# Hybrid decoder step on one core: inverses of four systems joined by products over a block diagonal, and decoding-state updates as one split product per head pair

## The chip, the cores and the metric

One core of a Trainium2 chip runs the whole kernel as one launch. The metric is the device time in microseconds. The numbers of before are three runs of the kernel, and one execution taken by the hardware profiler.

## The reference

One inference step of a decoder layer for a prompt of 1024 tokens and for 8 decoding sequences of one token each (1032 columns, d_model 2048). One input projection feeds four groups of heads (A gated delta rule, B RWKV-7, C forgetting attention over a paged cache, D causal pooling); their gated outputs go through one output projection and a layer norm. All in fp32. Two parts matter here.

In the prompt, A and B are computed in 16 chunks of 64 tokens for 8 heads each, and each chunk and head needs the inverse of a unit lower triangular 64x64 matrix (in the reference a triangular solve):

```python
tri = lower + eye
u = lax.linalg.triangular_solve(tri, vb, left_side=True, lower=True)
```

For the decoding sequences each head has a 64x64 state, decayed and then changed by outer products: one term for A (key x new value), two for B (key x value, and a x the state's reading).

```python
S = (S * w_t[:, :, None, :] + s_kk[..., :, None] * (kk_t * a_t)[:, :, None, :]
     + v_t[..., :, None] * k_t[:, :, None, :])
```

## The kernel before

The projections are products in a split format: each fp32 operand is split into a part rounded to the F32R format and a remainder, and three products per tile are accumulated (`mm3`, L308 to L310; "split format" below). 57 column tiles are projected one after the other, 16 k-tiles deep, in three column groups of 344.

All other work is written as generators that are *fillers* (`add`, `fill`): after each quarter of a tile's k-tiles (36 matmuls of the projection) every filler is advanced by its rate, so a `yield` is where a filler hands back to the projection. What a step issues is then ordered by the framework, which simulates a timeline and places each instruction on its engine's in-order queue where its operands are ready by that simulation; so a filler's product can end up behind projection matmuls that were written after it. DMAs issued as `nc.sync` share the SP queue, in order.

`inverses` (L1192) handles a branch in two pairs of head pairs (four heads, 16 chunks each), through `invert` (L1134). The 64x64 matrix is cut into 32x32 blocks. The two diagonal blocks of 4 heads and 16 chunks are loaded with (block, chunk) on the 128 partitions, inverted by 31 elimination steps on VectorE (L1155 to L1162, seven yields), and written to the operand tensor in DRAM (AOP or BOP). Then for each head, 4 per pair, the off-diagonal block -D1 C D0 is made: Uc and Ct are loaded with rows on 32 partitions, Uc is transposed by VectorE (L1176), 16 fp32 products of 32x32 with 32 rows (L1179), a negated copy by ScalarE (L1180), 16 more products (L1183), a copy (L1185) and the stores, one of them zeros. A *block* in this text is such a run of 16 products. Branch B's inverses and then its decoding step (`start_b`) run beside the projection of the A tiles, branch A's inverses (`cached`) beside that of the first C tiles, where `chain_b` runs as well.

`state_step` (L1421) decays the states (128 partitions for two heads, 8 sequences x 64 columns, for each of 4 head pairs), and for each term transposes key and value to rows (L1435, 8 partitions), spreads the value rows to a block diagonal over the 8 sequences (L1446), and multiplies in fp32: per head pair two products of 8 rows, 64 columns of weights and 512 streamed columns (L1447). VectorE adds the result to the states (L1448). It runs for B beside the A projection (tag "k", one PSUM buffer), for A in the second pass of the output projection (`sample_a`, tag "b", two buffers).

Other lines that the prediction names: L997 is decode's product of cached keys (weights 128x32, four column groups of the array, 256 streamed columns); L1504 and L1505 are a head sum in the split format (128 rows, 128 columns of weights, 512 streamed); L463 and L479 are small products of A's preparation.

Of the kernel before, what the change touches and what calls it, by code (L numbers as in the profile page):

```python
# [179 lines left out]
class Kernel:  # L180
# [953 lines left out]
    def invert(self, pool, br, pair):  # L1134
# [4 lines left out]
        ld = self.ld[br]  # L1139

# [5 lines left out]
        for hp in (2 * pair, 2 * pair + 1):  # L1146
            for hb in range(4):
                r = slice(32 * hb, 32 * hb + 32)
                b = slice(32 * (hb % 2), 32 * (hb % 2) + 32)
                nc.sync.dma_start(L[16 * q:16 * q + 16], ld[hp, r, :, b].rearrange("j c i -> c j i"))  # L1150
                dst[q] = OP[:, r, hp, off + b.start:off + b.stop]
                q += 1
        nc.gpsimd.memset(U, 0.0)
# [11 lines left out]
        for hp in (2 * pair, 2 * pair + 1):  # L1165
            X = self.t(pool, [128, 16, 32], "ivX", bufs=1)
            T1 = self.t(pool, [128, 16, 32], "ivT", bufs=1)
            Uc = self.t(pool, [128, 16, 32], "ivC", bufs=1)
            Ct = self.t(pool, [128, 16, 32], "ivD", bufs=1)
            f2 = lambda a: a.rearrange("p a b -> p (a b)")  # L1170
            for hh in range(2):
                p0, p1 = slice(64 * hh, 64 * hh + 32), slice(64 * hh + 32, 64 * hh + 64)
                nc.sync.dma_start(Uc[p0], OP[:, p0, hp, off:off + 32].rearrange("c p i -> p c i"))
                nc.sync.dma_start(Uc[p1], OP[:, p1, hp, off + 32:off + 64].rearrange("c p i -> p c i"))
                nc.sync.dma_start(Ct[p0], ld[hp, p0, :, 32:64])
                nc.vector.transpose(f2(T1[p0]), f2(Uc[p0]))  # L1176
                ps = self.ps("k")
                for c in range(16):
                    nc.tensor.matmul(ps[p1, 32 * c:32 * c + 32], lhsT=Ct[p0, c], rhs=T1[p0, c], start=True, stop=True)  # L1179
                nc.scalar.activation(f2(X[p1]), ps[p1], AF.Copy, scale=-1.0)  # L1180
                ps = self.ps("k")
                for c in range(16):
                    nc.tensor.matmul(ps[p0, 32 * c:32 * c + 32], lhsT=X[p1, c], rhs=Uc[p1, c], start=True, stop=True)  # L1183

                nc.scalar.copy(f2(T1[p0]), ps[p0])  # L1185
                nc.sync.dma_start(OP[:, p0, hp, off + 32:off + 64].rearrange("c p i -> p c i"), T1[p0])
                nc.gpsimd.memset(T1[p1], 0.0)
                nc.sync.dma_start(OP[:, p1, hp, off:off + 32].rearrange("c p i -> p c i"), T1[p1])
                yield True


    def inverses(self, br, **side):  # L1192
        with self.tc.tile_pool(reuse_waits="tile", name="inv" + br, bufs=1, **side) as pool:
            for pair in range(2):
                yield from self.invert(pool, br, pair)
# [226 lines left out]
    def state_step(self, pool, St, dec, terms, out, tag):  # L1422

        nc = self.nc
        blk = self.ident[0:8, 0:8].unsqueeze(2).to_broadcast([8, 8, 64])
        f = lambda a: a.rearrange("p b d -> p (b d)")
        for hp in range(4):
            nc.vector.tensor_tensor(St[:, hp], St[:, hp], dec[:, hp].unsqueeze(2).to_broadcast([128, 8, 64]), op=ALU.mult)
        yield True
        for k, v in terms:  # L1430
            kv = []
            for i, x in enumerate((k, v)):
                ps = self.ps(self.stag)
                for hp in range(4):
                    nc.tensor.transpose(ps[0:8, 128 * hp:128 * hp + 128], x[:, hp], self.ident)  # L1435
                r = self.t(pool, [128, 512], f"srow{i}", bufs=1)[0:8]
                nc.scalar.copy(r, ps[0:8])
                kv.append(r)
            kr, vr = kv
            yield True  # L1440
            for hp in range(4):
                ps = self.ps(self.stag)
                for hh in range(2):
# [489 lines left out]
```

## Time and profile before

| | |
|---|---|
| median of 3 runs | 2431.46 us (2424.43 to 2431.7) |
| profiled execution | 2431.75 us, span 2430.0 us, mean granted TensorE clock 0.979 |
| TensorE (PE) busy | 2330.0 us, 96% of the span, 18324 matmul records |
| weight loads (PEld) | 2055.6 us, 85% |
| VectorE (DVE) | 1371.7 us, 56% |
| ScalarE (ACT) | 940.3 us, 39% |
| GpSimd (POOL) | 298.8 us, 12% |
| HBM read and written | 314.56 MB and 83.62 MB, 164 GB/s over the span |

PE is TensorE's matmuls; they are pipelined, so the recorded durations of neighbours overlap, and the busy time of a group is the time in which at least one of its records ran. L12 is line 12 of the kernel. An entry like `k<-ivT,ivD` is tile written <- tiles read; `32*32` is rows x columns of the weights, `32x32` the streamed operand. "Idle before" is the time in which the engine did nothing just before those instructions, with what it waited for.

### The profile page before, as it was taken

The page shows a single profiled execution, that of the slowest core. Times are in us where ns is not written, and L with a number is a line of the kernel's source. Part 1 is how long each engine was busy: PE and PEld are TensorE (multiplying, and loading weights), DVE is VectorE, ACT ScalarE, POOL GpSimd, SP SyncE. Part 2 cuts the span into 40 slices and gives each one's busy share as a digit, 9 for nine tenths or more (in the row PEclk, how much of TensorE's full clock was granted, in tenths as well). Part 3 has the DMA queues.
Part 4 walks back from the last instruction along what each step waited for, and adds up shares of the span by engine and source line. Part 5 has one row for each costly group of instructions (what it writes and reads, how often), then busy time and mean ns, then how long its engine had stood idle before and what let it go on. Part 6 is the DMA issues. An engine that isn't in the chain of part 4 may idle for free. (4 is left out here: it accounts for less than half of the span.)

```text
span 2430.0 us, 48607 instructions
## 1 busy us (share of the span) xinstructions
PE 2330.0 (96%) x18324; PEld 2055.6 (85%) x18324; DVE 1371.7 (56%) x2677; ACT 940.3 (39%) x1861; POOL 298.8 (12%) x416
## 2 busy tenths in 40 slices
PE   8999999999999999999999999999999989999984
PEld 8999999999988999897777777999855579878984
DVE  4665667777465567522222244554588654564598
ACT  5644445434443444221111122553466665201244
POOL 0000000000000000112112111100122110100175
PEclk9999999999999999999999999999999999999997
DMA  6233433545432345878888888553398785783312
GB/s 215 52 107 88 111 87 93 150 92 111 109 79 66 92 105 127 181 191 259 268 266 280 278 282 300 187 159 79 111 277 240 230 299 161 216 299 116 91 65 87
DMA packets 368388, 401.46 MB, mean 165 GB/s; under 512 B 203853, under 2 KB 227326, under 8 KB 367386
## 3 DMA queue, kind: packets, MB, share of 16 engines
q1 hardware_dynamic: 306418, 262.78, 36.8%
q10 hardware_dynamic: 50056, 101.60, 14.9%
q0 software_dynamic: 11680, 33.99, 4.1%
q8 instruction: 144, 2.36, 0.4%
q14 instruction: 90, 0.74, 0.1%
HBM read 314.56 MB, written 83.62 MB: 164 GB/s over the span
## 5 line engine op out<-in xcount | busy, mean ns | idle before, releaser
L308 PE MATMUL pj<-xh,wlo 128*128 128x344 f32 x2688 | 875.2, 327 | 9.6 <-DVE wlo L303 8.2
L309 PE MATMUL pj<-xl,whi 128*128 128x344 f32 x2688 | 871.6, 324 | 0.0
L310 PE MATMUL pj<-xh,whi 128*128 128x344 f32 x2688 | 867.1, 324 | 0.0
L308 PEld LDWEIGHTS pj<-xh,wlo 128*128 128x128 f32 x2688 | 508.9, 189 | 38.2 <-issue 18.6
L309 PEld LDWEIGHTS pj<-xl,whi 128*128 128x128 f32 x2688 | 509.5, 190 | 19.0 <-issue 13.6
L310 PEld LDWEIGHTS pj<-xh,whi 128*128 128x128 f32 x2688 | 508.6, 190 | 16.7 <-issue 13.4
L302 ACT CAST whi<-raw 128x256 fp32r<-128x256 f32 (+1 forms) x504 | 213.0, 424 | 751.8 <-PE pj L310 515.6
L303 DVE TENSOR_TENSOR wlo<-raw,whi 128x256 fp32r<-128x256 f32 (+1 forms) x504 | 224.6, 448 | 393.0 <-ACT whi L302 380.3
L308 PE MATMUL o<-gh,wlo 128*128 128x344 f32 x576 | 184.9, 325 | 3.2 <-ACT gh L1662 2.6
L309 PE MATMUL o<-gl,whi 128*128 128x344 f32 x576 | 187.0, 325 | 0.0
L310 PE MATMUL o<-gh,whi 128*128 128x344 f32 x576 | 186.5, 324 | 0.0
L308 PEld LDWEIGHTS o<-gh,wlo 128*128 128x128 f32 x576 | 108.2, 189 | 26.1 <-DVE y L1687 8.5
L309 PEld LDWEIGHTS o<-gl,whi 128*128 128x128 f32 x576 | 109.6, 190 | 3.9 <-issue 2.5
L310 PEld LDWEIGHTS o<-gh,whi 128*128 128x128 f32 x576 | 109.8, 191 | 3.3 <-issue 3.3
L365 ACT ACTIVATE stg<-pj 128x344 f32<-128x344 f32 x168 | 74.7, 457 | 90.2 <-PE pj L310 89.1
L997 PE MATMUL k<-dkv,dqb 128*32 128x256 f32 x1024 | 90.6, 394 | 13.4 <-DMA dkv<-in_ck 12.9
L1687 DVE TENSOR_TENSOR y<-y,o 128x344 f32<-128x344 f32 x96 | 48.3, 509 | 68.0 <-PE o L310 67.8
L861 DVE TENSOR_TENSOR cpl<-cpt,cph 128x512 fp32r<-128x512 f32 (+1 forms) x96 | 61.7, 660 | 16.2 <-ACT cph L860 15.4
L1105 PE MATMUL k<-dkv,dpT 128*8 128x512 f32 x512 | 69.8, 621 | 0.4 <-DMA dkv<-in_cv 0.4
L308 PE MATMUL o<-gh,wkl 128*128 128x392 f32 (+2 forms) x192 | 63.8, 332 | 0.3 <-DVE wkl L303 0.2
L310 PE MATMUL o<-gh,wkh 128*128 128x392 f32 (+2 forms) x192 | 63.6, 331 | 0.0
L309 PE MATMUL o<-gl,wkh 128*128 128x392 f32 (+2 forms) x192 | 63.3, 330 | 0.0
(594 smaller groups left out, 3405.9 us busy)
## 6 DMA issues: line engine op xcount, KB each, us to landing
dkv<-in_ck SPq DMA_DIRECT2D x256, 256.0 KB
dkv<-in_cv SPq DMA_DIRECT2D x256, 256.0 KB
raw<-in_w ACTq DMA_DIRECT2D x228, 256.0 KB
out_pj<-stg ACTq DMA_DIRECT2D x33, 516.0 KB
bop<-bop SPq DMA_DIRECT2D x16, 1024.0 KB
raw<-in_wo ACTq DMA_DIRECT2D x64, 256.0 KB
aop<-aop SPq DMA_DIRECT2D x16, 768.0 KB
aop<-aost SPq DMA_DIRECT2D x40, 256.0 KB
```

The costliest lines, as they stand in the source:

```text
L302: nc.scalar.copy(hi, raw)
L303: nc.vector.tensor_tensor(lo, raw, hi.bitcast(F32), op=ALU.subtract)
L308: nc.tensor.matmul(ps, lhsT=wlo, rhs=xh, start=start, stop=False)
L309: nc.tensor.matmul(ps, lhsT=whi, rhs=xl, start=False, stop=False)
L310: self.last = nc.tensor.matmul(ps, lhsT=whi, rhs=xh, start=False, stop=stop).ins
L365: self.nc.scalar.activation(dst[:, g * G3:g * G3 + G3], ps[g], func)
L861: nc.vector.tensor_tensor(pl[:, off:], pt[:, off:], ph[:, off:].bitcast(F32), op=ALU.subtract)
L997: nc.tensor.matmul(ps[32 * hp:32 * hp + 32], lhsT=qb[:, hp, b], rhs=kt[:, :, hp], start=b == 0, stop=b == 7)
L1105: mm = lambda i: nc.tensor.matmul(po[32 * i:32 * i + 8], lhsT=pTv[:, c, :, 4 * bg + i], rhs=t[i // 2][:, i % 2], start=False, stop=c == 31)
L1687: nc.vector.tensor_tensor(y[:, s], y[:, s], ps[g], op=ALU.add)
```

## The change

Both parts of the diff follow. In `invert`, the off-diagonal blocks of all four heads of a pair are made together. The four heads' first diagonal inverses are put on the diagonal of a 128x128 matrix per chunk (BD, 16 chunks, zero elsewhere, allocated and cleared once per branch). As the first product needs them transposed, ScalarE writes U in another order over L, and the blocks go through a scratch tensor in DRAM (UT) back into BD. One product per chunk, with the four heads' off-diagonal blocks stacked on 128 partitions as weights (128x32), gives all four heads; the chunk index modulo 4 picks the output partitions, that is the column group of the array. After a negated copy, the diagonal of BD is overwritten with the second inverses, arranged by chunk modulo 4 (sixteen DMAs), and a second set of 16 products ends it. The zero block is stored from a part of BD off its diagonal.

In `state_step`, the rows of keys and values are made by ordinary fp32 products with the identity, three copies of 16 rows (two heads x 8 sequences) at partitions 0, 32 and 64. From them come a rounded part and, in one of the three copies (the second for keys, the third for values), the remainder, so that one product over 80 rows in the split format gives the three terms hi*hi, lo*hi and hi*lo. The two heads of a pair are in one product of 128 columns of weights and 512 streamed columns.

```diff
--- before.py
+++ after.py
@@ -1131,12 +1131,13 @@
             nc.sync.dma_start(self.lfd[4 * i:4 * i + 4].rearrange("b g f -> (b g) f"), t)
 
 
-    def invert(self, pool, br, pair):
+    def invert(self, pool, br, pair, BD):
 
 
         nc = self.nc
         OP, off = (self.AOP, 320) if br == "A" else (self.BOP, 448)
         ld = self.ld[br]
+        heads = [(hp, hh) for hp in (2 * pair, 2 * pair + 1) for hh in range(2)]
 
         L = self.t(pool, [128, 32, 32], "ivL", bufs=1)
         U = self.t(pool, [128, 32, 32], "ivU", bufs=1)
@@ -1150,6 +1151,10 @@
                 nc.sync.dma_start(L[16 * q:16 * q + 16], ld[hp, r, :, b].rearrange("j c i -> c j i"))
                 dst[q] = OP[:, r, hp, off + b.start:off + b.stop]
                 q += 1
+
+        Ct = self.t(pool, [128, 16, 32], "ivD", bufs=1)
+        for q, (hp, hh) in enumerate(heads):
+            nc.sync.dma_start(Ct[32 * q:32 * q + 32], ld[hp, 64 * hh:64 * hh + 32, :, 32:64])
         nc.gpsimd.memset(U, 0.0)
         nc.gpsimd.memset(U.rearrange("p c i -> p (c i)")[:, ::33], 1.0)
         for j in range(31):
@@ -1162,37 +1167,49 @@
                 yield True
         for q in range(8):
             nc.sync.dma_start(dst[q], U[16 * q:16 * q + 16])
-        for hp in (2 * pair, 2 * pair + 1):
-            X = self.t(pool, [128, 16, 32], "ivX", bufs=1)
-            T1 = self.t(pool, [128, 16, 32], "ivT", bufs=1)
-            Uc = self.t(pool, [128, 16, 32], "ivC", bufs=1)
-            Ct = self.t(pool, [128, 16, 32], "ivD", bufs=1)
-            f2 = lambda a: a.rearrange("p a b -> p (a b)")
-            for hh in range(2):
-                p0, p1 = slice(64 * hh, 64 * hh + 32), slice(64 * hh + 32, 64 * hh + 64)
-                nc.sync.dma_start(Uc[p0], OP[:, p0, hp, off:off + 32].rearrange("c p i -> p c i"))
-                nc.sync.dma_start(Uc[p1], OP[:, p1, hp, off + 32:off + 64].rearrange("c p i -> p c i"))
-                nc.sync.dma_start(Ct[p0], ld[hp, p0, :, 32:64])
-                nc.vector.transpose(f2(T1[p0]), f2(Uc[p0]))
-                ps = self.ps("k")
-                for c in range(16):
-                    nc.tensor.matmul(ps[p1, 32 * c:32 * c + 32], lhsT=Ct[p0, c], rhs=T1[p0, c], start=True, stop=True)
-                nc.scalar.activation(f2(X[p1]), ps[p1], AF.Copy, scale=-1.0)
-                ps = self.ps("k")
-                for c in range(16):
-                    nc.tensor.matmul(ps[p0, 32 * c:32 * c + 32], lhsT=X[p1, c], rhs=Uc[p1, c], start=True, stop=True)
-
-                nc.scalar.copy(f2(T1[p0]), ps[p0])
-                nc.sync.dma_start(OP[:, p0, hp, off + 32:off + 64].rearrange("c p i -> p c i"), T1[p0])
-                nc.gpsimd.memset(T1[p1], 0.0)
-                nc.sync.dma_start(OP[:, p1, hp, off:off + 32].rearrange("c p i -> p c i"), T1[p1])
-                yield True
-
+
+        nc.scalar.copy(L, U.rearrange("p c i -> p i c"))
+        for q in range(4):
+            nc.sync.dma_start(self.UT[q], L[32 * q:32 * q + 16])
+        yield True
+        for q in range(4):
+            nc.sync.dma_start(BD[32 * q:32 * q + 32, :, 32 * q:32 * q + 32], self.UT[q].rearrange("c p i -> p c i"))
+        yield True
+
+        ps = self.ps("k")
+        for c in range(16):
+            m, n = c % 4, c // 4
+            nc.tensor.matmul(ps[32 * m:32 * m + 32, 128 * n:128 * n + 128], lhsT=Ct[:, c], rhs=BD[:, c], start=True, stop=True)
+        X = self.t(pool, [128, 4, 4, 32], "ivX", bufs=1)
+        nc.scalar.activation(X.rearrange("p n q i -> p (n q i)"), ps, AF.Copy, scale=-1.0)
+
+        for m in range(4):
+            b = slice(32 * m, 32 * m + 32)
+            for q, (hp, hh) in enumerate(heads):
+                p1 = slice(64 * hh + 32, 64 * hh + 64)
+                nc.sync.dma_start(BD[b, q::4, b], OP[m::4, p1, hp, off + 32:off + 64].rearrange("c p i -> p c i"))
+        yield True
+        ps = self.ps("k")
+        for n in range(4):
+            for q in range(4):
+                nc.tensor.matmul(ps[32 * q:32 * q + 32, 128 * n:128 * n + 128], lhsT=X[:, n, q], rhs=BD[:, 4 * n + q],
+                                 start=True, stop=True)
+        T1 = self.t(pool, [128, 16, 32], "ivD", bufs=1)
+        nc.scalar.copy(T1.rearrange("p c i -> p (c i)"), ps)
+        for q, (hp, hh) in enumerate(heads):
+            p0, p1 = slice(64 * hh, 64 * hh + 32), slice(64 * hh + 32, 64 * hh + 64)
+            nc.sync.dma_start(OP[:, p0, hp, off + 32:off + 64].rearrange("c p i -> p c i"), T1[32 * q:32 * q + 32])
+
+            z = 32 * ((q + 1) % 4)
+            nc.sync.dma_start(OP[:, p1, hp, off:off + 32].rearrange("c p i -> p c i"), BD[32 * q:32 * q + 32, :, z:z + 32])
+        yield True
 
     def inverses(self, br, **side):
         with self.tc.tile_pool(reuse_waits="tile", name="inv" + br, bufs=1, **side) as pool:
+            BD = self.t(pool, [128, 16, 128], "ivB", bufs=1)
+            self.nc.gpsimd.memset(BD, 0.0)
             for pair in range(2):
-                yield from self.invert(pool, br, pair)
+                yield from self.invert(pool, br, pair, BD)
 
     def act_table(self):
 
@@ -1422,29 +1439,45 @@
     def state_step(self, pool, St, dec, terms, out, tag):
 
         nc = self.nc
-        blk = self.ident[0:8, 0:8].unsqueeze(2).to_broadcast([8, 8, 64])
         f = lambda a: a.rearrange("p b d -> p (b d)")
+
+
+        rows = slice(0, 80)
+        blk = self.c("selb")[rows].unsqueeze(2).to_broadcast([80, 8, 64])
         for hp in range(4):
             nc.vector.tensor_tensor(St[:, hp], St[:, hp], dec[:, hp].unsqueeze(2).to_broadcast([128, 8, 64]), op=ALU.mult)
         yield True
         for k, v in terms:
             kv = []
             for i, x in enumerate((k, v)):
+                two = self.t(pool, [128, 4, 2, 8, 2], "stw", bufs=1).rearrange("p h a b t -> p (h a b t)")[:, 0:64]
+                nc.gpsimd.memset(two, 0.0)
+                two = two.rearrange("p (h a b) -> p h a b", h=4, a=2)
+                for hh in range(2):
+                    r = slice(64 * hh, 64 * hh + 64)
+                    nc.vector.tensor_copy(two[r, :, hh], x[r])
                 ps = self.ps(self.stag)
                 for hp in range(4):
-                    nc.tensor.transpose(ps[0:8, 128 * hp:128 * hp + 128], x[:, hp], self.ident)
-                r = self.t(pool, [128, 512], f"srow{i}", bufs=1)[0:8]
-                nc.scalar.copy(r, ps[0:8])
-                kv.append(r)
+                    for b in range(3):
+                        nc.tensor.matmul(ps[32 * b:32 * b + 16, 128 * hp:128 * hp + 128],
+                                         lhsT=two[:, hp].rearrange("p a b -> p (a b)"), rhs=self.ident, start=True, stop=True)
+                r = self.t(pool, [128, 512], f"srow{i}", F32R, bufs=1)[rows]
+                nc.vector.tensor_scalar(r, self.onec[rows].to_broadcast([80, 512]), 0.0, None, op0=ALU.mult)
+                for b in range(3):
+                    s = slice(32 * b, 32 * b + 16)
+                    nc.scalar.copy(r[s], ps[s])
+                    if b == 1 + i:
+                        nc.vector.tensor_tensor(r[s], ps[s], r[s].bitcast(F32), op=ALU.subtract)
+                kv.append(r.rearrange("p (h a d) -> p h a d", h=4, a=2))
+                yield True
             kr, vr = kv
-            yield True
+            fv = vr.bitcast(F32)
+            nc.vector.tensor_tensor(vr[:, :, 0], fv[:, :, 0], fv[:, :, 1], op=ALU.add)
             for hp in range(4):
+                bd = self.t(pool, [128, 8, 64], "sbd", F32R, bufs=1)[rows]
+                nc.vector.tensor_tensor(bd, fv[:, hp, 0].unsqueeze(1).to_broadcast([80, 8, 64]), blk, op=ALU.mult)
                 ps = self.ps(self.stag)
-                for hh in range(2):
-                    cs = slice(128 * hp + 64 * hh, 128 * hp + 64 * hh + 64)
-                    bd = self.t(pool, [128, 8, 64], "sbd", bufs=1)[0:8]
-                    nc.vector.tensor_tensor(bd, vr[:, cs].unsqueeze(1).to_broadcast([8, 8, 64]), blk, op=ALU.mult)
-                    nc.tensor.matmul(ps[64 * hh:64 * hh + 64], lhsT=kr[:, cs], rhs=f(bd), start=True, stop=True)
+                nc.tensor.matmul(ps, lhsT=kr[:, hp].rearrange("p a d -> p (a d)"), rhs=f(bd), start=True, stop=True)
                 nc.vector.tensor_tensor(f(St[:, hp]), f(St[:, hp]), ps, op=ALU.add)
                 yield True
         nc.gpsimd.dma_start(out, St)
@@ -1759,6 +1792,7 @@
         self.cs8 = tc.dram_tile([8, T], F32, name="cs8")
         self.gr = tc.dram_tile([8, N], F32, name="grow")
         self.br = tc.dram_tile([8, N], F32, name="brow")
+        self.UT = tc.dram_tile([4, 16, 32, 32], F32, name="ut")
         self.lfd = tc.dram_tile([8, 32, 1024], F32, name="lfd")
         self.crow = tc.dram_tile([8, 4, T], F32, name="crow")
         self.sco = tc.dram_tile([128, 4097], F32, name="sco")
```

## Rows read from the trace of the kernel before

**Rows 1.** Windows: us, busy us (records) of PE, PEld, DVE, ACT, POOL, clock, DMA share

```profile
500.00:700.00 200.00, 195.52 (x1868) 187.70 (x1867) 137.46 (x329) 88.17 (x178) 9.02 (x20) 0.96 0.46 100
900.00:1100.00 200.00, 195.11 (x2320) 180.64 (x2319) 106.62 (x258) 59.43 (x127) 26.40 (x46) 0.99 0.72 170
2100.00:2200.00 100.00, 100.00 (x602) 80.75 (x602) 60.02 (x96) 13.97 (x22) 1.32 (x2) 1.00 0.79 266
```

**Rows 2.** Groups by line and shape, PE: busy, mean ns of one, idle before

```profile
L1179 PE MATMUL k<-ivT,ivD 32*32 32x32 f32 x512 | 20.7, 195 | 2.3 <-DVE ivT L1176 1.7 <-ACT asq L1205 0.6
...
L1183 PE MATMUL k<-ivC,ivX 32*32 32x32 f32 x512 | 19.5, 192 | 2.8 <-ACT ivX L1180 2.8
...
L1447 PE MATMUL k<-sbd,srow 8*64 8x512 f32 x32 | 17.1, 613 | 0.0
```

**Rows 3.** Timeline of PE: start us, us, what, count; a block among projection matmuls

```profile
565.43 1.19 PE L1183 MATMUL k<-ivC,ivX 32*32 32x32 f32 x32
566.56 0.43 PE L310 MATMUL pj<-xh,whi 128*128 128x344 f32 x1
566.82 0.32 PE L308 MATMUL pj<-xh,wlo 128*128 128x344 f32 x1
```

**Rows 4.** Timeline of PE: a row transpose, and a product of the state update

```profile
703.23 0.60 PE L1435 MATMUL k<-cst,sxs 128*8 128x128 f32 x4
...
703.82 0.32 PE L308 MATMUL pj<-xh,wlo 128*128 128x344 f32 x1
...
709.32 0.31 PE L310 MATMUL pj<-xh,whi 128*128 128x344 f32 x1
709.57 1.07 PE L1447 MATMUL k<-sbd,srow 8*64 8x512 f32 x2
710.57 0.43 PE L308 MATMUL pj<-xh,wlo 128*128 128x344 f32 x1
710.83 0.32 PE L309 MATMUL pj<-xl,whi 128*128 128x344 f32 x1
```

**Rows 5.** Timeline of PE: second product of a head sum, and the projection behind it

```profile
671.91 0.39 PE L1505 MATMUL b<-hsh,bonesr 128*128 128x512 f32 x1
672.14 0.32 PE L308 MATMUL pj<-xh,wlo 128*128 128x344 f32 x1
672.30 0.32 PE L309 MATMUL pj<-xl,whi 128*128 128x344 f32 x1
```

**Rows 6.** Windows, columns as in Rows 1: four stretches with inverse blocks

```profile
552.00:560.00 8.00, 6.94 (x59) 6.39 (x58) 6.47 (x12) 2.20 (x5) 0.10 (x1) 0.79 1.10 148
584.00:596.00 12.00, 10.53 (x96) 10.16 (x94) 9.05 (x22) 6.43 (x13) 1.04 (x2) 0.86 0.34 65
616.00:632.00 16.00, 14.96 (x217) 14.17 (x215) 8.72 (x14) 8.09 (x15) 0.00 (x0) 0.68 0.57 136
995.00:1000.00 5.00, 5.00 (x22) 4.81 (x22) 1.45 (x7) 1.27 (x3) 0.14 (x1) 0.66 1.02 242
```

**Rows 7.** Timeline of PE: the first block of the kernel, a projection matmul after it

```profile
553.52 1.19 PE L1179 MATMUL k<-ivT,ivD 32*32 32x32 f32 x32 [1.06 <-DVE ivT L1176]
...
555.40 0.49 PE L308 MATMUL pj<-xh,wlo 128*128 128x344 f32 x1
```

**Rows 8.** Timeline of PE: products of cached keys, and the projection behind them

```profile
1204.54 0.64 PE L997 MATMUL k<-dkv,dqb 128*32 128x256 f32 x8
1205.11 0.43 PE L308 MATMUL pj<-xh,wlo 128*128 128x344 f32 x1
```

**Rows 9.** Who waited for line L1173, a load of Uc: us, times

```profile
  DVE ivT L1176: 12.0, 6
```

**Rows 10.** Line L1164, the stores of U: issue on SP, ns min/median/max

```profile
L1164 SPq DMA_DIRECT2D bop<-ivU x16: 303/534/904, 542.7 to 608.9; - x16
```

**Rows 11.** Groups by line and shape, DVE and ACT, of the state update

```profile
L1446 DVE TENSOR_TENSOR sbd<-srow,cst 8x512 f32<-8x512 f32 x24 | 16.2, 675 | 13.9 <-PE k L1447 9.1 <-ACT srow L1437 4.7
...
L1437 ACT COPY srow<-k 8x512 f32<-8x512 f32 x4 | 2.3, 574 | 4.3 <-PE k L1435 4.3
```

## The prediction

> **What bounds the kernel now.** Three views, in this order. First the busy time by stretch [rows 1]: TensorE is busy 195.5, 195.1 and 100.0 us of 200, 200 and 100 us in the stretches that hold the work the change touches, VectorE 137, 107 and 60, ScalarE 88, 59 and 14. So here the time is the sum of what is queued on TensorE, and a filler's product lengthens the kernel by what it takes of TensorE, not by its own chain. Second the groups by line and shape [rows 2]: each fp32 product is recorded as two instructions, so 512 records at the inverses' two lines are 256 products each, that is 16 blocks of 16 products at each line, 32 blocks in all; the state updates are 24 products (32 of their 48 records, those in tile k, are the row shown). Mean durations overlap (512 x 195 ns is not 20.7 us), so costs are read from the third view, the timeline: start to start, against the projection's own pace beside it.
>
> **What the inverses cost now.** A block of 32 records starts at 565.43 and the next projection matmul at 566.56: 1.13 us, 35 ns a record [rows 3]. Around it the pace is broken: 0.25 us from the last projection matmul to a filler's fp32 product [rows 4], 0.26 us from the first one after a block to the next, where undisturbed neighbours are 0.16 apart [rows 5]; so 0.19 us more a block. Not every block stands between projection matmuls, and I take 0.15. 32 x 1.28 = 41 us. TensorE also stood still in front of these blocks, 2.3 + 2.8 = 5.1 us [rows 2]. And the granted clock fell around some of them: four stretches have 0.79, 0.86, 0.68 and 0.66 [rows 6], which over 8, 12, 16 and 5 us are 1.7 + 1.7 + 5.1 + 1.7 = 10.2 us of full-speed time. What came before the first fall is 1.06 us idle and one 32x32 block; two microseconds later a projection matmul is recorded with 0.49 us [rows 7] in place of 0.32 [rows 4], the lower of the two levels, 1.2 instead of 2.4 GHz.
>
> **What they cost after.** Each pair of head pairs has two blocks of 16 products (32 records) instead of eight: 8 blocks in place of 32. A product is now 128 rows deep, 32 columns of weights wide and streams 128 columns, and the 16 go round four column groups of 32. No row has this shape. The nearest is the cached-key product, the same weights and the same four groups with 256 streamed columns: 8 records in 0.57 us, 71 ns each [rows 8]. Half the columns would be 35 ns, which is also the pace of the present 32x32 records; so 1.13 us a block from below and, if fewer columns gained nothing, 2.3 from above. If the column groups didn't overlap at all, the price would follow the state update's 512-column records, two in 1.00 us [rows 4]: 0.125 for 128 columns, 4.0 us a block. I take 1.13, as the overlap is in the nearest row: 8 x (1.13 + 0.19) = 10.6 us.
>
> New waits. Before, a load went to VectorE's transpose, which waited 12.0 us in 6 waits for it [rows 9], 2.0 us each, and TensorE came behind; now the first product takes its operand straight from a load that is itself behind a write (inverse to a scratch tensor, back onto the diagonal), and the second waits for sixteen loads. Issue on the SP queue is 0.534 us for such a DMA [rows 10], so these sixteen take 8.5 us. Other matmuls can stand in between, as now: 2.8 us idle in front of sixteen blocks that each wait for a ScalarE copy [rows 2]. I take 1.0 us of idle TensorE a block, 8 us; the ends are 0 and 2.0 (16 us). For the clock I take four falls of 1.7, 6.8 us, since the blocks stay few and short and fill all rows; the ends are none and eight (13.6). Inverses: 41 + 5.1 + 10.2 - 10.6 - 8 - 6.8 = 31 us gained.
>
> **The state updates.** Now: from the last projection matmul before a product to the second after it are 1.51 us [rows 4], two ordinary steps are 0.31, so 1.20 us each and 28.8 for 24. The transposes that make the rows: from 703.23 to the second projection matmul after them 0.59, less one step of 0.16 = 0.43 a block [rows 4], six blocks, 2.6 us. After: 12 products in the split format, 80 rows deep, 128 columns of weights, 512 streamed. The head sum has this format and width: its second product takes 0.23 us to the next start and the projection goes on without a break [rows 5]; 12 x 0.23 = 2.8 us. The rows are now made six times by 12 ordinary fp32 products of 128 columns (24 records) on three column groups: 24 x 35 ns x 4/3 = 1.13 us, plus 0.19, 7.9 us in all; ends 0.85 (35 ns) and 1.7 (71 ns) a block. Gained: 31.4 - 10.7 = 21 us.
>
> **What I cost at nothing, and its cover.** VectorE loses 16 transposes and per term four of eight block-diagonal products of 0.675 [rows 11], and gets four small copies, two clears, two subtractions and an addition over up to 512 columns, about the same sum; ScalarE loses 24 of 32 evacuations of the inverses, of the width that takes 0.574 in the row copies [rows 11], and gets four row copies more per term, 12 x 0.574 = 7 us, and a reordering copy of 1024 columns per pair, about 1.2 each. Both have a quarter or more of every stretch free [rows 1]; without that cover the worst is the 7 us. The generators yield about as often (11 steps per pair, as before; one more in the row making per operand), so what is handed out with which projection chunk moves little. SP gets 16 DMAs more per pair, 8.5 us of issue each, 34 us over both stretches, in front of the loads of the next preparation steps; TensorE has the projections to go on with, so nothing waits unless a preparation step is late. The clear of the block matrix and the small clears are GpSimd's, which is busy 9 of 200 us.
>
> **Sum.** Against the profiled execution, 2431.75 us (span 2430.0): 31 + 21 = 52 us less, 2380. The median of the runs shown, 2431.46, is the same within 0.3 us, so 2380 stands. With no stall and no fall of the clock it is 2365, with both upper ends 2395.
>
> **A page to weigh.** Rows first: a copy of 512 columns out of PSUM is 0.574 us on 8 partitions [rows 11], which I take for 16 and 128 too, and TensorE stood idle 0.0 us in front of the updates that follow the row copies [rows 2]. The Trainium skill, TensorEngine Tiling (Array Packing), section Performance Considerations, says that packing speeds the products but not the way out of PSUM, which may become the bottleneck, and that both ScalarE and VectorE should share it. By it the three row copies and a subtraction, in line on one bank, would be the new limit, and the sum would be about 16 us worse. The rows speak against it, as here projections fill the gap; its result is the second rival below.
>
> **Rivals.**
> 1. The column groups don't overlap: 4.0 us a block and 3.0 us for the rows add 8 x 2.9 + 6 x 1.9 = 35: 2415. Against it: 8 records of 256 columns in 0.57 us can't be done one by one.
> 2. The copies out of PSUM hold TensorE: three copies of 0.574 and a VectorE step of 0.675 in place of one copy, 1.82 us more, six times, and 0.574 after each of eight inverse blocks: 11 + 4.6 = 16 us, 2396. For it: tile k has one buffer. Against it: the idle times of [rows 2].
> 3. The loads decide: in each pair TensorE stands for the sixteen loads, 8.5 us, and 2.0 us for the first product, and the clock falls eight times: 42 + 13.6 against the 14.8 in my sum, 41 us worse: 2421. For it: the 12.0 us that VectorE waited. Against it: the projection matmuls that can stand in between.
> 4. Where DMA is busy, time freed on TensorE turns into waiting for pages and operands: share 0.72 and 0.79 in two of the stretches [rows 1]. Half of the inverses' gain (15) and a third of the updates' (7) go: 2402.
> 5. Slower: the whole chain from the end of the elimination to the second product stands in front of TensorE, because the order puts the products at once behind it: 32 DMAs of 0.534 and two landings of 2.0 are 21 us a pair, 84 in all, against 66 gained without stalls: 2449. It decides from 16.6 us a pair (66.4/4). Against it: no wait in front of the present blocks adds up to more than 2.8 us in 16.
>
> **How the numbers follow.** Forecast 0.70, with its own range 2365 to 2395; rivals 1 to 5: 0.06, 0.08, 0.08, 0.05, 0.03. Below 2360 more would have to go than I can find; above 2412 lie rivals 1, 3 and 5. So 2360 to 2412 leaves out less than 2 in 10. What this kernel's measurement can tell from no change is 0.3%, 7.3 us: all cases but the fifth lie beyond it on the fast side; with something for a miss that I don't see, faster 0.94, same 0.03, slower 0.03.
>
> **What would show it.** Right: the inverses' two lines with 128 records each, about 1.1 us from a block's start to the projection after it; the update at 0.23 us a product with no gap; granted clock in the first stretch at 0.98 or more; TensorE busy some 50 us less and its idle share unchanged. Wrong: idle time before the inverse blocks with a load as releaser of more than 2 us a block (rival 3), blocks of 3 us (rival 1), idle time at the row products or updates ended by ScalarE (rival 2), more idle before the cached pages' products in the stretch at 2100 us (rival 4).

## The result and the profile after

| | before | after | forecast |
|---|---|---|---|
| median | 2430.9 us (2431.46 in the runs shown ahead) | 2397.8 us (2390.03 to 2401.3) | 2380 (2360 to 2412) |
| ratio | | 0.9871, 95% interval 0.9848 to 0.9895 | 0.979 |
| profiled execution: time, span, clock | 2431.75, 2430.0, 0.979 | 2396.94, 2395.2, 0.979 | |

Faster, as forecast, by 33 us where 52 were forecast: inside the range, 3 us outside the likeliest case's own range. The page of the profile after, first row:

```profile
PE 2282.6 (95%) x17640; PEld 2023.0 (84%) x17640; DVE 1364.7 (57%) x2676; ACT 938.4 (39%) x1853; POOL 295.0 (12%) x408
```

TensorE is busy 47.4 us less (some 50 were forecast), but its share fell from 96% to 95%: part of what it no longer computes it now waits. The stretches of [rows 1] in the changed kernel, same columns, with three short ones behind them:

```profile
500.00:700.00 200.00, 189.59 (x1580) 179.33 (x1579) 142.27 (x348) 91.25 (x183) 7.40 (x20) 0.98 0.49 107
900.00:1100.00 200.00, 187.87 (x1915) 168.76 (x1914) 92.42 (x238) 51.67 (x111) 28.23 (x48) 0.98 0.73 175
2100.00:2200.00 100.00, 100.00 (x639) 87.95 (x638) 59.49 (x91) 11.27 (x19) 0.55 (x1) 1.00 0.67 233
...
636.00:640.00 4.00, 2.13 (x14) 1.85 (x12) 0.90 (x2) 0.14 (x1) 1.75 (x4) 1.00 0.99 332
640.00:644.00 4.00, 0.23 (x1) 0.23 (x2) 0.77 (x2) 1.78 (x5) 0.00 (x0) 0.89 0.90 90
644.00:648.00 4.00, 4.00 (x15) 4.00 (x16) 3.46 (x10) 2.19 (x8) 0.00 (x0) 0.50 0.22 67
```

Idle time in the first rose from 4.5 to 10.4 us, in the second from 4.9 to 12.1. The products themselves, groups of PE by line and shape (answers to [rows 2]; L1182 and L1195 are the inverses' two products, L1462 the rows of keys and values, L1480 the updates):

```profile
L1195 PE MATMUL k<-ivB,ivX 128*32 128x128 f32 x128 | 9.8, 278 | 4.0 <-DMA ivB<-bop 2.7 <-DMA ivB<-aop 1.0 <-issue 0.3
...
L1182 PE MATMUL k<-ivB,ivD 128*32 128x128 f32 x128 | 5.8, 310 | 7.2 <-DMA ivB<-ut 6.9 <-DMA raw<-in_w 0.3
...
L1462 PE MATMUL k<-cst,stw 128*16 128x128 f32 x96 | 4.2, 274 | 0.0
...
L1480 PE MATMUL k<-sbd,srow 80*128 80x512 f32 x8 | 3.3, 413 | 0.0
```

The same number of records at both inverse lines, but product 2 takes 4 us more and both have idle time ended by loads. The timeline shows how (PE, SP's queue and ScalarE; in brackets the idle time before an instruction and what ended it; answers to [rows 3 to 5] and [rows 10]):

```profile
556.49 1.08 PE L1182 MATMUL k<-ivB,ivD 128*32 128x128 f32 x32
557.50 0.43 PE L308 MATMUL pj<-xh,wlo 128*128 128x344 f32 x1
...
562.99 8.98 SPq L1190 DMA_DIRECT2D ivB<-bop  x16
...
571.92 0.38 PE L1195 MATMUL k<-ivB,ivX 128*32 128x128 f32 x2 [2.09 <-DMA ivB<-bop]
572.23 0.42 PE L309 MATMUL pj<-xl,whi 128*128 128x344 f32 x1
572.59 0.41 PE L1195 MATMUL k<-ivB,ivX 128*32 128x128 f32 x2
...
574.28 1.06 PE L1195 MATMUL k<-ivB,ivX 128*32 128x128 f32 x26
575.27 0.43 PE L308 MATMUL pj<-xh,wlo 128*128 128x344 f32 x1
...
620.01 9.06 SPq L1190 DMA_DIRECT2D ivB<-bop  x16
632.94 1.09 SPq L407 DMA_DIRECT2D aogb<-grow  x2
...
642.22 0.63 ACT L442 ACTIVATE aoeg<-aogb 128x512 f32<-128x512 f32 x1 [6.09 <-DMA aogb<-grow]
643.77 0.66 PE L308 MATMUL pj<-xh,wlo 128*128 128x344 f32 x1 [5.64 <-ACT stg L365]
...
703.35 0.40 PE L1480 MATMUL k<-sbd,srow 80*128 80x512 f32 x1
703.59 0.32 PE L308 MATMUL pj<-xh,wlo 128*128 128x344 f32 x1
```

An undivided block costs 1.01 us from its start to the projection (forecast 1.13), an update 0.24 (forecast 0.23) with no gap behind it. But product 2 first waits 2.09 us for its sixteen loads, and then its first records come two at a time between projection matmuls and the last 26 in one run. Each change costs: from 572.23 to 572.59 are 0.36 us, where undisturbed projection matmuls start 0.16 apart. Behind the second block ScalarE stands 6.09 us for a load, TensorE 5.64 for ScalarE, and then runs for some 4 us at 0.50, the lower level of its clock (the window from 644 above). What TensorE waited for from 500 to 1110 us (total, times, longest):

```profile
PE k L1182 <- DMA ivB<-ut: 6.9, 2, 4.6
PE pj L308 <- ACT stg L365: 5.6, 1, 5.6
PE k L1195 <- DMA ivB<-bop: 2.7, 2, 2.1
```

To tell the terms apart I added up, from windows of 4 us between 12 us (where the matmuls begin) and 2280 us, TensorE's idle time and its full-speed time lost to the clock (4 us x (1 - granted clock)); *work* is the rest of the span's difference, with the tail behind 2280 us. The sums are good to some tenths. The rows are differences to before, from one profiled execution each, and not always a typical one: e1's is 7 us and e8's 6 us above the median of its runs, e6's 3 us below. The experiments follow below.

| kernel | span | idle (before: 51.6) | clock (before: 32.5) | work |
|---|---|---|---|---|
| forecast (whole time) | -52 | +2.9 | -3.4 | -51 |
| after | -34.8 | +13.8 | -1.8 | -46.8 |
| after, run again (e12) | -34.4 | +14.5 | -3.6 | -45.3 |
| new inverses only (e1) | +5.0 | +17.3 | +11.8 | -24 |
| new state updates only (e2) | -15.6 | +8.6 | -5.2 | -19 |
| after, without the sixteen loads (e5) | -40.9 | +13.5 | -3.5 | -51 |
| after, without any trip through DRAM (e6) | -55.5 | +5.4 | -12.1 | -49 |
| after, sixteen loads twice (e8) | +0.4 | +27.6 | +22.0 | -49 |

Work is what was forecast, within 2 to 6 us. Idle time is not, and the kernels with more of it also lose more to the clock. Each fall of the clock cost 1.7 us or a multiple of it: 19 times 1.7 before, 18 times after.

### The profile page after: what moved, and what is told of

Its sections match the earlier page's. It is cut to its first block, busy times and chain, and to the rows that moved or that the text cites. A ratio compares the mean times of both kernels' runs of the same rounds, so it can differ in the third digit from the quotient of the medians.

```text
span 2395.2 us, 47251 instructions
## 1 busy us (share of the span) xinstructions
PE 2282.6 (95%) x17640; PEld 2023.0 (84%) x17640; DVE 1364.7 (57%) x2676; ACT 938.4 (39%) x1853; POOL 295.0 (12%) x408
## 3 DMA queue, kind: packets, MB, share of 16 engines
HBM read 314.56 MB, written 84.67 MB: 167 GB/s over the span
## 5 line engine op out<-in xcount | busy, mean ns | idle before, releaser
L997 PE MATMUL k<-dkv,dqb 128*32 128x256 f32 x1024 | 88.4, 394 | 15.1 <-DMA dkv<-in_ck 9.0
```

Source lines behind the costliest of these rows:

```text
L997: nc.tensor.matmul(ps[32 * hp:32 * hp + 32], lhsT=qb[:, hp, b], rhs=kt[:, :, hp], start=b == 0, stop=b == 7)
```

## Experiments

Ratios are to the kernel before, run beside each group. *Trips* are the ways of the diagonal inverses through DRAM: to UT and back (four stores, four loads a pair) and the sixteen loads. The kernel before had loads of the same size: Uc came in 32 loads of 64 KB, in pieces of 128 bytes; now it is 16 loads of 64 KB and 64 of 16 KB, in the same pieces. So the number of small packets is nearly unchanged (pages of before and after), and both kernels read 314.56 MB:

```profile
DMA packets 368388, 401.46 MB, mean 165 GB/s; under 512 B 203853, under 2 KB 227326, under 8 KB 367386
...
DMA packets 369664, 402.44 MB, mean 168 GB/s; under 512 B 204877, under 2 KB 228350, under 8 KB 368666
```

**e1 and e2, the two halves alone.** e1 keeps the old `state_step`, e2 the old `invert`.

```diff
 # e1, against the changed kernel: state_step as before
-                nc.tensor.matmul(ps, lhsT=kr[:, hp].rearrange("p a d -> p (a d)"), rhs=f(bd), start=True, stop=True)
+                    nc.tensor.matmul(ps[64 * hh:64 * hh + 64], lhsT=kr[:, cs], rhs=f(bd), start=True, stop=True)
...
 # e2, against the changed kernel: invert and inverses as before
-            nc.tensor.matmul(ps[32 * m:32 * m + 32, 128 * n:128 * n + 128], lhsT=Ct[:, c], rhs=BD[:, c], start=True, stop=True)
+                    nc.tensor.matmul(ps[p1, 32 * c:32 * c + 32], lhsT=Ct[p0, c], rhs=T1[p0, c], start=True, stop=True)
...
```

> The inverses in the new form, the state updates in the old one. Theory L (loads: the inverse part gave less than forecast because TensorE stands for the new loads and for what waits behind them on the SP queue): 12 us below before, 2419, with 9 to 12 us of idle in front of the two inverse lines. Rival S (the state part is what gave less, as its row copies hold TensorE): the full 31 us, 2400.

> The state updates in the new form, the inverses in the old one. Theory L: the full 21 us below before, 2410, with no idle at the row products or the updates. Rival S: 5 us or less, 2426, with idle ended by ScalarE.

e1: 2429.7 us, ratio 0.9992 (0.9976 to 1.0008). e2: 2414.5, 0.9929 (0.9914 to 0.9944). The updates give 17 us alone, near the 21 forecast, and rival S, that their copies hold TensorE, is out. In e2's profile 8.6 of the 19 us of work came back as idle time, 5 of them from 1700 to 2280 us. The inverses, forecast at 31, give nothing alone, which neither theory had: in the profiled execution their work is gone (-24 in the table) and comes back as idle time and clock, 8.6 us of it in front of the two inverse lines.

**e3, the loads on GpSimd's queue.** All 20 loads onto the diagonal are issued there, so nothing stands behind them on SP.

```diff
-            nc.sync.dma_start(BD[32 * q:32 * q + 32, ...
+            nc.gpsimd.dma_start(BD[32 * q:32 * q + 32, ...
...
-                nc.sync.dma_start(BD[b, q::4, b], ...
+                nc.gpsimd.dma_start(BD[b, q::4, b], ...
```

> The changed kernel with the twenty loads per pair that fill the block matrix issued from GpSimd, not from the SP queue. Theory L with the queue as the cause: SP no longer carries 11 us of issue in front of the preparation's stores and loads, the stall of 5.6 us on an evacuation and the 1.7 us on a preparation product go, and half of the 11.2 us in front of the inverse products: 2386. Rival D (the 16 DMA engines are busy, whoever issues): the same as the changed kernel, 2398, with the waits in place.

2397.6 us, 0.988 (0.9859 to 0.9901): no change. Waits of TensorE from 500 to 1110 us in this kernel:

```profile
PE a L479 <- ACT aost L466: 5.4, 1, 5.4
PE a L1352 <- ACT bvs L1347: 4.7, 1, 4.7
PE pj L308 <- ACT stg L365: 2.9, 2, 2.1
PE k L1182 <- DMA bvs<-bop: 2.2, 1, 2.2
```

The waits at product 2 are gone and others of the same size have opened at lines that were not touched. Idle time as a whole, from 12 to 2280 us, is 12.3 us above before, where the changed kernel has 13.8: SP's order decided who waits more than how long.

**e4, one more hand-back before each product.**

```diff
+        yield True
         ps = self.ps("k")
```

> The changed kernel with one more yield in front of each of the two inverse products, so that one more projection chunk lies between the loads and the product. Theory L with the product's own wait as the cause: the 11.2 us in front of the two lines fall under 3, and a fall or two of the clock with them: 2388; the 5.6 us on an evacuation may stay. If what is behind the loads on SP is the larger part: 2394 or no change, 2398.

2397.1 us, 0.9853 (0.9829 to 0.9876): the second of the two expected cases. In its trace the products wait 6.6 and 4.1 us for their loads, as in the changed kernel (6.9 and 2.7). One more hand-back in the program did not bring the products behind their loads.

**e5, e6 and e8, a ladder of trips.** e5 leaves out the sixteen loads; e6 also the stores to UT and the loads from it, so that both products read zeros; e8 issues the sixteen loads twice.

```diff
 # e5 and e6
-                nc.sync.dma_start(BD[b, q::4, b], OP[m::4, p1, hp, off + 32:off + 64]...
 # e6
-            nc.sync.dma_start(self.UT[q], L[32 * q:32 * q + 16])
-            nc.sync.dma_start(BD[32 * q:32 * q + 32, :, 32 * q:32 * q + 32], self.UT[q]...
 # e8
+        for twice in range(2):
             for m in range(4):
```

> Leaves out the sixteen loads of every inverse block (64 in all), so product 2 takes the transposed blocks that lie in the buffer already; everything else stays. Changed kernel: 2397.8 us. Theory L (the sixteen loads cost: 9.0 us of SP's queue a block, during which stores and loads of the projection stand behind them, and product 2's wait for them): the waits at product 2 (2.7 + 1.0 us) and the two stalls behind the queue (1.65 and 5.64 us, the latter with 3.4 us of half clock) go, some 11 to 14 us: 2385, at most 2388. Rival G (the new idle comes from the schedule: TensorE's work is gone and what it waits for arrives no earlier, so other waits open): at least two thirds comes back elsewhere, 2393 to 2399.

> As the kernel without the sixteen loads, and leaves out the way of the transposed blocks through DRAM as well (four stores and four loads a block, 32 in all): the products read a buffer of zeros and wait for no load but that of Ct. Theory L, waits on the loads: the 6.9 us of idle in front of product 1 go as well, together with the half clock behind the 4.58 us wait: 2373 to 2380. Rival G: 2388 to 2396, with new waits at other lines.

> Issues the sixteen loads of each block twice (the same data). Theory L: SP's queue holds 18 us a block instead of 9 and the last load lands some 9 us later, product 2 and the stores and loads behind wait that much longer where nothing covers it: two of the four blocks show such stalls now, so 2405 to 2420. Rival G (the loads lie beside other work and the waits at them are only where idle shows): 2396 to 2401.

| trips | none (e6) | without the sixteen loads (e5) | as changed | sixteen loads twice (e8) |
|---|---|---|---|---|
| median, us | 2379.6 | 2388.9 | 2397.8 | 2425.7 |
| ratio | 0.9794 (0.9771 to 0.9817) | 0.9816 (0.9792 to 0.9841) | 0.9871 (0.9848 to 0.9895) | 0.9977 (0.9958 to 0.9996) |

The two trips cost 18 us together (15 by the ratio of the changed kernel's second measurement, e12), and 64 loads of 16 KB more cost 28. That e6 comes out at the forecast's 2380 is a coincidence: this sum has 14.8 us of waits and falls of the clock in it, and without them the prediction had 2365. So even with no trip 15 us are missing; in e6's profile idle time is 5.4 us above before, although the 5.1 in front of the old blocks are gone. Rival G, that other waits open in their place, is right for a part: e5 has as much idle time as the changed kernel (13.5 and 13.8), only at other lines, and gains because product 2 is undivided (4.7 us instead of 9.8) and by the clock.

Two reservations. e5, e6 and e11 leave out loads that the kernel before had too: e6 reads 312.46 MB where before reads 314.56. So they show what the operands' way costs, not what the change added to it. And e6 and e11 multiply zeros, and the chains behind get other numbers; whether that matters to the clock no run shows.

e6's product groups and its stretches, to be read beside those of after:

```profile
L1178 PE MATMUL k<-ivB,ivD 128*32 128x128 f32 x128 | 5.9, 279 | 1.2 <-DMA ivD<-ldA 1.2
L1186 PE MATMUL k<-ivB,ivX 128*32 128x128 f32 x128 | 4.7, 276 | 0.0
```

```profile
500.00:700.00 200.00, 195.42 (x1650) 185.98 (x1649) 150.36 (x362) 97.51 (x194) 7.29 (x20) 1.00 0.46 102
900.00:1100.00 200.00, 191.54 (x2076) 167.99 (x2074) 92.64 (x240) 48.25 (x105) 29.54 (x49) 0.98 0.77 204
```

5.9 + 4.7 = 10.6 us of busy time, beside the forecast's 10.6, which is counted from start to start and with the broken pace; undivided, product 2 takes 4.7 where it took 9.8. Idle time in the first stretch is back at 4.6 us and the clock is at 1.00. In e8 product 2 waits three times as long, 8.4 us of it for nothing that the profile shows (its group, and SP's queue):

```profile
L1196 PE MATMUL k<-ivB,ivX 128*32 128x128 f32 x128 | 9.0, 286 | 13.3 <-issue 8.4 <-DMA ivB<-bop 2.5 <-DMA raw<-in_w 2.4
```

```profile
564.96 16.25 SPq L1191 DMA_DIRECT2D ivB<-bop  x32
```

**e7, four loads instead of sixteen.** The second inverses are also stored to a scratch array in the order of product 2, and come back in four loads of 64 KB; it computes the same.

```diff
+            nc.sync.dma_start(self.U2[:, q], U[32 * q + 16:32 * q + 32])
...
-            m, n = c % 4, c // 4
+            m, n = c // 4, c % 4
...
-                nc.sync.dma_start(BD[b, q::4, b], OP[m::4, p1, hp, off + 32:off + 64]...
+            nc.sync.dma_start(BD[b, :, b], self.U2[4 * m:4 * m + 4]...
```

> Computes the same: the lower inverses are also stored to a scratch array in the order in which product 2 reads them (four more stores a block, early), and the sixteen loads become four of 64 KB (a load of that size from the other scratch array took 0.5 to 0.75 us of SP's queue); chunks are dealt to column groups by quarter. If SP's queue is what counts: 9.0 us of issue become 2.5, the stalls of 1.65 and 5.64 us behind it shrink, 2388 to 2391. If the landing or the moved bytes count (the same 1 MB a block, plus 0.25 MB stored): 2396 to 2400. Rival G: 2395 to 2399.

2406.5 us, 0.989 (0.9869 to 0.9911): no better. But the edit did two things. To get the new order it also deals the chunks out by quarters, so that product 1 runs four products in a row on one column group, where the changed kernel goes round all four. A block of it, undivided:

```profile
560.42 2.43 PE L1183 MATMUL k<-ivB,ivD 128*32 128x128 f32 x32 [0.79 <-DMA ivB<-ut]
562.78 1.15 PE L463 MATMUL a<-cst,aoeg 64*64 64x64 f32 x32
```

From start to next start it takes 2.36 us instead of 1.01, and product 1 is busy 14.0 us in all instead of 5.8. Without these 8.2 us I estimate 2398 for e7, the changed kernel's time. What was to be taken away did go: SP's queue is held for 2.6 us instead of 9, and product 2 waits 1.1 us in all. Other waits took its place (SP's queue, and TensorE's waits from 500 to 1110 us):

```profile
565.59 2.62 SPq L1189 DMA_DIRECT2D ivB<-u  x4
```

```profile
PE pj L308 <- ACT stg L365: 13.1, 4, 5.5
PE k L1183 <- DMA ivL<-ldA: 6.5, 1, 6.5
PE k L1183 <- DMA ivB<-ut: 6.0, 3, 4.6
PE k L1194 <- DMA ivB<-u: 1.1, 1, 1.1
```

With e3 this speaks against the theory that SP's queue is what costs, though e7 is no clean test of it. What all these kernels keep is many small pieces to move. The changed kernel's DMA view from 600 to 660 us (queue: packets, MB, share of the 16 engines; q1 is SP's queue, q10 ScalarE's, with the weights):

```profile
DMA packets 18148, 6.74 MB, mean 112 GB/s; under 512 B 16592, under 2 KB 16656, under 8 KB 18016
...
q1 hardware_dynamic: 16832, 3.68, 35.2%
q10 hardware_dynamic: 1008, 1.84, 9.8%
```

SP's queue took 9.6% per MB, the weights' 5.3%. The Trainium skill, DMA: Bandwidth & Descriptors, section Specifications, says that transfers under 512 bytes miss the full rate; by that rule cutting the number of DMAs and not the size of their pieces gains nothing, and this trace agrees, as does e7 once product 1's price is taken off. No run here changed the size of the pieces, so that it is these that cost is argued, not shown. Nor does their number tell the kernels apart, since the kernel before moved as many. What did change is that a pair's loads now come in one burst, and that each of the two products needs all of its loads; that this is the reason is argued too.

**e9 and e10, the stall of 5.64 us.** e9 starts B's decoding step later; e10 also stores the zero blocks in the middle of the elimination.

```diff
         yield from self.inverses("B")
+        for _ in range(3):
+            yield True
```

> Three more yields between the inverses of branch B and the first loads of branch B's decoding step (1 MB on GpSimd's queue), some 15 us; the step ends well within its stage. Theory C (collision): the 5.64 us stall at 643.77 comes from these loads, issued at 633 to 637, which share the DMA engines (0.89 to 1.21 busy) with the four stores of the zero blocks and the gate rows that ScalarE waits for 6.1 us. Apart, the stall and the 3.4 us at half clock behind it go: 2387 to 2391. Theory L (the gate rows stood behind the sixteen loads in SP's queue): the stall stays, 2395 to 2399.

> As the kernel with the three yields, and the four stores of the zero blocks (64 KB each, 16 in all) are issued in the middle of the elimination instead of behind product 2. Theory C: they leave the tail of every block, where chain B's and the projections' loads wait for the same DMA engines: 2 to 5 us under the kernel with the yields alone, 2383 to 2388. If the late loads of the decoding step were all of it: the same as that kernel within 1.5 us.

e9: 2395.5 us, 0.9852 (0.9829 to 0.9874). e10: 2396.7, 0.9864 (0.9844 to 0.9884). Beside the changed kernel run again with them (e12) neither gained. The edit moved the step's loads by little: they start 1.17 us behind the gate rows' load on SP (L407), where it was 0.28 us in the changed kernel and 0.40 in e12. Yet that was enough for the place: e9's two loads, its windows, and TensorE's waits for the projection's copy from 500 to 1110 us:

```profile
634.63 1.10 SPq L407 DMA_DIRECT2D aogb<-grow  x2
635.80 0.57 POOL L1616 DMA_DIRECT2D sS<-in_sB  x1 [60.76 <-PE k L1195]
...
640.00:644.00 4.00, 2.61 (x17) 2.33 (x16) 1.92 (x6) 3.45 (x9) 0.32 (x2) 1.00 1.05 256
644.00:648.00 4.00, 4.00 (x27) 4.00 (x26) 3.47 (x9) 1.40 (x5) 0.00 (x0) 1.00 0.27 73
```

```profile
PE pj L308 <- ACT stg L365: 2.8, 2, 1.5
```

The stall shrank from 5.6 us (5.7 in e12) to 1.4 and the half-speed stretch behind it is gone, as theory C, a collision of loads, expects for the place; it is one execution, and no view shows which load delayed which. And what was won there did not reach the end: against e12's profile, e9 has 4.9 us less idle time from 500 to 1110 us and as much lost clock (6.8), and from there to 1700 us 3.7 us more idle and 3.4 more lost to the clock. Why it came back is not settled.

**e11, the new inverses without trips, old state updates.**

```diff
 # e1, and as in e6
-                nc.sync.dma_start(BD[b, q::4, b], OP[m::4, p1, hp, off + 32:off + 64]...
-            nc.sync.dma_start(self.UT[q], L[32 * q:32 * q + 16])
-            nc.sync.dma_start(BD[32 * q:32 * q + 32, :, 32 * q:32 * q + 32], self.UT[q]...
```

> The new inverses with the old state updates, and without the transposed blocks' way through DRAM and the sixteen loads (products read zeros). Theory T (the trips through DRAM are all that the inverses' half fell short by): 31 us under before, 2399, between 2395 and 2404. Rival I (the half is worth less without the other edit, as 2429.7 with the trips had it against 2414.5 and 2397.8): 2408 to 2416.

2394.9 us, 0.9853 (0.9827 to 0.9878): 35 us under before, where theory T had 31. Rival I is wrong: the inverses' half gains without the other edit too, if its operands come for nothing. But theory T's 31 has waits and falls in it as well; without them the prediction's terms give 46 (41 + 5.1 + 10.2 - 10.6), so 11 us are missing here too. Its stretches:

```profile
500.00:700.00 200.00, 197.48 (x1607) 185.25 (x1606) 147.98 (x351) 94.19 (x189) 6.84 (x17) 0.99 0.44 102
900.00:1100.00 200.00, 192.52 (x2084) 170.26 (x2085) 95.76 (x247) 51.77 (x111) 29.48 (x50) 1.00 0.78 200
```

**e12, the changed kernel again.** No edit.

> The changed kernel once more, for its time and clock beside the others on this chip: 2397.8, within 3 us. If it comes out at 2391 or lower, the gains of the two kernels with moved loads are to be counted from there.

2395.7 us, 0.9854 (0.9831 to 0.9878), beside e9 to e11. No version beat the changed kernel with the same computation.

## Why the prediction was right and where it failed

**Right.** The removed work (47 of 51 us), the price of the new products (1.13 us a block, measured 1.01 undivided) and the updates (0.24 us each, no gap; the half alone 17 of 21 us). Rivals 1 and 2 fell with these rows: 32 records in 1.01 us are not one after the other, as e7's 2.36 us for four in a row on one group shows beside it, and idle time before the updates in tile k is 0.0, so the rule of the Trainium skill's page on tiling (TensorEngine Tiling (Array Packing), Performance Considerations) did not bind here: the projections fill the gap. That the time fell into the range owes something to the range's width: 2397.8 is nearer to rivals 2 (2396) and 4 (2402) than to 2380.

Rival 4 was placed wrongly: the cached pages' products (L997) run from 1096 to 1527 us in the kernel before, none of them at 2100 us, where TensorE is busy 100.00 of 100 us before and after. Where they run, their wait for pages from 1110 to 1700 us was 12.9 us before, 9.0 after and 12.5 in e12. Its idea, that freed time turns into waiting, is what e1 and a part of e2 show, but at other lines.

**Wrong: the term for new waits.** The prediction wrote "I take 1.0 us of idle TensorE a block, 8 us", with 16 as its upper end, on the ground that other matmuls can stand in between. Measured, idle time rose by 13.8 us net; with the 5.1 us in front of the old blocks that went, that is 18.9, beyond the upper end. In front of the blocks themselves stand 11.2 us of it (7.2 + 4.0), 1.4 a block where 1.0 was taken. The largest single wait was not before a block at all but 5.64 us before a projection matmul, behind ScalarE. That was the gap in the reasoning: SP's load was costed at nothing because "TensorE has the projections to go on with", while the projections' own evacuation runs on ScalarE, and ScalarE waited 6.09 us for a load on SP's queue while the DMA engines were 0.99 busy. A second, smaller piece is work: product 2 is busy 9.8 us with its sixteen loads and 4.7 without them, since every change between it and the projection breaks the pace, which I had counted once a block. A third piece had no term at all: freed time that turns into waiting at lines no edit touched, as in e2 and e6. In e6's profile it is 10.5 us (5.4 + 5.1) of what is missing to 2365; what causes it was not found.

**The clock.** Forecast 3.4 us better, 1.8 better in the profiled pair. From 500 to 1110 us, where the inverses run, 10.3 us were lost before and 6.8 after, which is the forecast's 10.2 and 6.8; but half of the 6.8 lies behind ScalarE's stall, which the forecast did not have, so the fit is partly luck. The rest is lost later, 22.2 us before and 23.9 after. Over the 34 runs of before beside e1 to e8 the mean granted clock was 0.9816, over 8 runs of after 0.9791, so on the whole it got worse: 2430 x 0.0184 = 45 us lost before and 2396 x 0.0209 = 50 after. Without trips it was 0.9818, with doubled loads 0.9727. So the trips cost twice, as idle time and as clock.

**Rival 3** (the loads decide, 2421) named a cause that is there, at too high a price: it had product 1's wait about right (2.0 us a pair, 7.2 in all), but product 2 waits 4.0 us in all, not 8.5 a pair, and the trips cost 18 us, not 41. Only with twice the loads (e8, 2425.7) does the time come near its figure, and there product 2 waits 13.3 us.

**Open.** With the old updates the trips cost 34 us (e1 against e11), with the new ones 18. In e1's profile 26 steps of lost clock stand against 18, more than half of them from 1700 us on, where e1 changes no instruction; but its mean clock over the runs, 0.9782, is only 2 us worse than that of after. So the halves' gains do not add (0 + 17 against 33), and what couples them was not found.

## What to carry to other kernels

Fewer, larger products are priced well from rows of the nearest shape; what must be priced with them is the way their operands take. If loads that were spread over many small steps now come in one burst in front of one product, count the wait for all of them, and not only in front of that product: look for every load that shares the DMA engines, above all those that the evacuating engine waits for. To size such a term, leave the loads out and double them; taking away a single stall did not show it. And compare the run without them with the forecast without its waits, not with the forecast as a whole.

## What the runs showed of the hardware

- Sixteen fp32 products of 128 rows, 32 columns of weights and 128 streamed columns, dealt over four column groups, took 1.01 us, no more than the 1.13 us that sixteen of 32 rows and 32 columns took [rows 3]: four times the rows and the columns for the same time. It depends on the order: with four products in a row on one column group, and not one on each in turn, they took 2.36 us (e7).
- Issue on SP hardly depended on size here: 0.56 us for each of sixteen loads of 16 KB (8.98 us), 0.66 for each of four of 64 KB (2.62 us in e7). Yet with e3 and e7 the time of the kernel did not follow the time of issue.
- Time lost to the clock differs much in a stretch where nothing was changed: from 1700 to 2280 us, 15.4 us before, 17.1 after, 25.6 in e1, 13.6 in e6 and 34.1 in e8. All of it lies before 1972 us, and the one changed part in that stretch, A's state update, runs behind 2090 us.
